# Decay differences on GpSimd, a second buffer for exp(cum), and the second half's HGRN norm in pieces: one change to a two-layer SSD/HGRN2 trunk

## The chip, the cores and the metric

The kernel runs on one core of a Trainium2 chip. The metric is the device time of one execution in microseconds (us). The kernel before was timed in three runs: 2899.86, 2904.77 and 2904.81, median 2904.77. One further execution was profiled, and all rows of profile and trace come from that one.

## The reference

An encoder trunk of two layers, width D = 1024, runs one step over 1024 frames of a new stream (x_prompt) and 32 frames of a running one (x_sample) with the same weights. Layer 0 is a Mamba-2 SSD mixer, layer 1 an HGRN2 mixer; a SwiGLU follows each, and an rmsnorm stands ahead of each of the four and at the end. Cut to what matters:

```python
# SSD, one chunk of frames, per group of 8 heads (4 groups)
cum   = jnp.cumsum(dtc * Ag, axis=1)                  # running sum, never rising: A < 0
seg   = cum[:, :, None] - cum[:, None, :]             # cum_t - cum_s
decay = where(mask, exp(where(mask, seg, 0.0)), 0.0)  # causal: s <= t
xdt   = xc * dtc[..., None]
cb    = einsum('btgn,bsgn->btsg', Cc, Bc)
y = einsum('btsg,btsgh,bsghp->btghp', cb, decay, xdt)
y = y + einsum('btgn,bghpn->btghp', Cc, S) * exp(cum)[..., None]
S = exp(last) * S + einsum('bsgh,bsghp,bsgn->bghpn', exp(last - cum), xdt, Bc)
# gate: yg = (y + D*x) * silu(z), rmsnorm over a group, @ out_w
# HGRN2: h = rmsnorm(x, w); q, f, i, g = split(h @ in_w); gated linear recurrence per head (8 of 128);
#        rmsnorm over a head, * silu(g), @ out_w
```

For s <= t the difference cum_t - cum_s is never above 0, so the exponential may be taken of min(cum_t - cum_s, 0) for all pairs and masked afterwards.

## The kernel before

**Tiling.** Everything lies transposed: features on 128 partitions, frames on the free axis. The frames are cut into two halves: the first of 512 columns, the second of 544 (512 and the 32 of x_sample). Residuals, norms and weights live in SBUF as fp32; a matrix product is made as three passes on TensorE of numbers split into a high and a low part: L314 is high weight by high input, L315 high weight by low input, L316 low weight by high input. ScalarE copies raw weights to their high part (wh<-raw), VectorE subtracts to get the low one (wl<-raw,wh). ScalarE makes all exponentials, Tanh and copies out of PSUM; VectorE the products and sums. L98, L101, L104, L107 and L110 are the lines of the helpers act, tt, stt, ts and dma, so an operation is known by its tiles.

**SSD layer.** Loop over two halves, and in each over four groups of 8 heads. A group has four chunks of 128 frames (in the second half a fifth, of the 32 sample frames). For each chunk:

- `chunk_loads` (L524 on), issued one chunk ahead on SP's queue, brings cum of 8 heads, broadcast over partitions, into two tiles cumB (4 heads each, 128 x 512; tag "cb" of four buffers, so two chunks), and exp(cum) into ec (tag "ec", one buffer). The first chunk of the first half needs no ec.
- `ssd_chunk`: TensorE makes C by B (L552) and transposes x (L557); VectorE makes xdt and xw; ScalarE turns each head's 128 x 128 piece of cumB into a clamped difference with one Relu (scale -1, bias the column cum of the head), then takes one Exp per tile with scale -1; VectorE multiplies with the masked C by B. TensorE transposes B (L572) and ScalarE copies it (Btok, in the trace fixed<-sc 128x128); L579 is C by S, L582 the state product of Btok and xw, L593 the eight products of xdt with the decay tiles, after which the cumB buffers are free.

In the trace an instruction of ScalarE with cumB<-cumB,fixed is such a Relu, one with cumB<-cumB 128x512 the Exp. Among the chunks of a group stand *tasks*: the four z projections of the group (`ssd_z`: a Tanh by ScalarE out of PSUM, z<-mm, then a VectorE operation on it) and the output projections of the group before. After its last chunk comes the gate (`ssd_gate`: squares, a product with ones at L331, Ln, Exp), then the convolution tiles of the next group.

**HGRN layer.** 16 units: two halves, in each eight heads; a unit has four or five chunks (`hgrn_chunk`, `hgrn_chunk_b`, L806 to L825), a gate (`hgrn_gate`: square of the head's output ho, product with ones at L331, Ln, Exp = rstd, two VectorE products, the split into hy), and among its chunks tasks: its own g projection (hg), every second head the output projection of the two heads before (mm<-hy), and the f, q, v projections of the next head. Behind these, in head 6 of the first half, stands the norm of the second half (`norm(1, C_HGN, xns[1], XN2)`): eight squares by ScalarE with seven sums by VectorE, two products with ones (L331), Ln, Exp, and then for each of 8 row blocks a VectorE product, ScalarE's copy (h<-xf) and VectorE's low part.

**What sets the order.** Each engine runs its instructions in a fixed order, which a scheduler writes at build time from priorities and its own costs: program order, with some kinds lifted (L112: norm=600, gate=100, hchunk=50, others 0). Semaphores are placed accordingly. A lifted kind may stand far ahead of where it is written.

Of the kernel before, what the change touches and what calls it, by code (L numbers as in the profile page):

```python
# [11 lines left out]
AF = mybir.ActivationFunctionType  # L12
ALU = mybir.AluOpType
# [9 lines left out]
LEN = (H1, SEQ - H1 + NS)  # L23
# [14 lines left out]
C_SSDN, C_CB, C_FFN, C_HGN, C_GN, C_HG, C_LB = 0, 8, 32, 48, 56, 72, 73  # L38
# [2 lines left out]

TW = 552
FIXED = 14368
BUFS = {"x": 12, "ys": 8, "cb": 4, "xd": 2, "ec": 1, "ss": 1, "xr": 2, "n": 4, "w": 3}
WIDTH = {k: TW for k in BUFS}


@with_exitstack
def trunk_kernel(ctx, tc, x_prompt, x_sample, state_ssd, cache_conv, state_hgrn,
# [5 lines left out]
    V, A, G, PE = nc.vector, nc.scalar, nc.gpsimd, nc.tensor  # L55
# [17 lines left out]
    def slot(tag, s):  # L73
        return T(tag, s, F32R) if isinstance(tag, str) else tag
# [22 lines left out]
    def act(out, in_, f, **kw):  # L97
        A.activation(out=out, in_=in_, func=f, **kw)  # L98
# [7 lines left out]
    def ts(out, a, s1, s2, op0, op1, eng=None):  # L106
        (eng or V).tensor_scalar(out=out, in0=a, scalar1=s1, scalar2=s2, op0=op0, op1=op1)  # L107
# [17 lines left out]
    MUL, ADD, SUB = ALU.mult, ALU.add, ALU.subtract  # L125
# [41 lines left out]
    xr = place(9)  # L167
# [170 lines left out]
    XN = [xnt[:, i] for i in range(16)]  # L338
    XN2 = ["x"] * 12 + ["cb"] * 4
# [39 lines left out]
    @lifted("norm")  # L379
    def norm(h, wc, out, tags, blocks=None, r=None):  # L380

        for (b0, bn) in blocks or ((0, LEN[h]),):
            mmb = BLK[h] if blocks is None else [(0, bn)]
            if r is None:
                r = rstd_of([acc[h][m][:, b0:b0 + bn] for m in range(KD)], mmb, 1.0 / D, bn)
            for m in range(KD):
                xf = T("n", "xf")
                stt(xf[:, :bn], acc[h][m][:, b0:b0 + bn], vc[:, wc + m:wc + m + 1], r[:, :bn], MUL, MUL)
                if m == len(out):
                    out.append((slot(tags[2 * m], "h"), slot(tags[2 * m + 1], "l")))  # L390
                xh, xl = out[m]
                act(xh[:, b0:b0 + bn], xf[:, :bn], AF.Copy)
                tt(xl[:, b0:b0 + bn], xf[:, :bn], xh[:, b0:b0 + bn].bitcast(F32), SUB)
        return out
# [8 lines left out]
    st = [place(TW) for _ in range(NG)]  # L403
# [138 lines left out]
    @lifted("chunk")  # L542
    def ssd_chunk(h, g, c, S, loads, u):
        o, n, smp = CHUNKS[h][c]
        Bt, Ct, xs, Y = u["x"][0], u["x"][1], u["x"][2:], u["Y"]
        cols, elast = dts[h]
        xo = o + (3 if smp else 0)
        Bx, Cx = Bt[:, xo:xo + n], Ct[:, xo:xo + n]
        h0 = g * 8
        cums, ec = loads  # L550
        ps = psum_sc()
        PE.matmul(ps[:n, :n], Bx, Cx, start=True, stop=True)  # L552
        cbm = small("cbm")
        tt(cbm[:n, :n], ps[:n, :n], cmask[:n, :n], MUL)
        ps = psum_sc()
        for j in range(4):
            PE.transpose(ps[:n, j * P:(j + 1) * P], xs[j][:, xo:xo + n], ident)  # L557
        x3 = ps[:n, :].rearrange("p (h q) -> p h q", q=64)
        xdt, xw = T("xd", "xdt")[:, :512], T("xd", "xw")[:, :512]
        tt(xdt[:n, :].rearrange("p (h q) -> p h q", q=64), x3,  # L560
           cols[:n, c, h0:h0 + 8].unsqueeze(2).to_broadcast([n, 8, 64]), MUL)
        tt(xw[:n, :].rearrange("p (h q) -> p h q", q=64), x3,
           cols[:n, c, 64 + h0:64 + h0 + 8].unsqueeze(2).to_broadcast([n, 8, 64]), MUL)
        for q in range(2):
            cb3 = cums[q]
            for i in range(4):
                hh = 32 + h0 + 4 * q + i
                act(cb3[:n, i, :n], cb3[:n, i, :n], AF.Relu, scale=-1.0, bias=cols[:n, c, hh:hh + 1])
            act(cb3[:n, :, :n], cb3[:n, :, :n], AF.Exp, scale=-1.0)
            tt(cb3[:n, :, :n], cb3[:n, :, :n], cbm[:n, :n].unsqueeze(1).to_broadcast([n, 4, n]), MUL)  # L570
        ps = psum_sc()
        PE.transpose(ps[:n, :P], Bx, ident)  # L572
        Btok = small("Btok")
        act(Btok[:n, :], ps[:n, :P], AF.Copy)
        if ec is not None:
            y2 = psum_sc()
            y23 = y2.rearrange("p (j t) -> p j t", t=P)
            for j in range(4):
                PE.matmul(y23[:, j, :n], S[:, j * P:(j + 1) * P], Cx, start=True, stop=True)  # L579
            tt(ec[:, :, :n], y23[:, :, :n], ec[:, :, :n], MUL)  # L580
        pp = psum_sc()
        PE.matmul(pp, Btok[:n, :], xw[:n, :], start=True, stop=True)  # L582
        if ec is None:
            V.tensor_copy(S, pp)
        else:
            S3 = S.rearrange("p (h q) -> p h q", q=64)
            tt(S3, S3, elast[:, h0:h0 + 8, c:c + 1].to_broadcast([P, 8, 64]), MUL)
            tt(S, S, pp, ADD)
        y1 = psum_sc()
        y13 = y1.rearrange("p (j t) -> p j t", t=P)  # L590
        for i in range(8):
            r = 64 * (i % 2)
            PE.matmul(y13[r:r + 64, i // 2, :n], xdt[:n, i * 64:(i + 1) * 64], cums[i // 4][:n, i % 4, :n],  # L593
                      start=True, stop=True)
        yo = Y[:, :, o:o + n]
        if ec is None:
            act(yo, y13[:, :, :n], AF.Copy)
        else:
            tt(yo, y13[:, :, :n], ec[:, :, :n], ADD)
# [260 lines left out]
    def hgrn_layer(after):  # L860
        units = [(h, e) for h in range(2) for e in range(8)]
        us = [{"S": None} for _ in units]
        for f in (hgrn_f, hgrn_q, hgrn_v):
            f(0, 0, us[0])
        for i, (h, e) in enumerate(units):
            u = us[i]
            tasks = [lambda: hgrn_g(h, e, u)]
            if e % 2 == 0 and i:
                ph, pe = units[i - 1]
                tasks += [lambda m4=m4: hgrn_out(ph, pe // 2, m4, [us[i - 2]["y"], us[i - 1]["y"]])  # L870
                          for m4 in range(2)]
            if i + 1 < len(units):
                nh, ne = units[i + 1]
                tasks += [lambda f=f: f(nh, ne, us[i + 1]) for f in (hgrn_f, hgrn_q, hgrn_v)]
            if (h, e) == (0, 6):
                tasks.append(lambda: norm(1, C_HGN, xns[1], XN2))
            if (h, e) == (1, 6):
                tasks += after[:1]
            if (h, e) == (1, 7):
                tasks += after[1:]  # L880
            u["o"] = T("ys", "ho")
            if e % 2 == 0:
                yt = sp.tile([P, 4 * TW], F32R, tag="Y", bufs=1, name=nm("hy"))[:, :4 * LEN[1]]
                yp = yt.rearrange("p (j t) -> p j t", j=4)
            u["yp"] = yp
            nch = len(CHUNKS[h])
            for c in range(nch):
                second = hgrn_chunk(h, e, c, u)
                q = -(-len(tasks) // (nch - c))
                for i2, t in enumerate(tasks[:q]):  # L890
                    if i2 == HB2:
                        second()
                    t()
                if q <= HB2:
                    second()
                tasks = tasks[q:]
            hgrn_gate(h, e, u)
        return [lambda m4=m4: hgrn_out(1, 3, m4, [us[-2]["y"], us[-1]["y"]]) for m4 in range(2)]
# [6 lines left out]
    def x_stat(h, keep):  # L905

        return rstd_of([acc[h][m][:, :LEN[h]] for m in range(KD)], BLK[h], 1.0 / D, LEN[h], keep)

    def norm_pieces(h, wc, out, blocks, r):

        def piece(m, b0, bn):
            xf = T("n", "xf")
            stt(xf[:, :bn], acc[h][m][:, b0:b0 + bn], vc[:, wc + m:wc + m + 1], r[:, b0:b0 + bn], MUL, MUL)
            if m == len(out):
                out.append((XN[2 * m], XN[2 * m + 1]))
            xh, xl = out[m]
            act(xh[:, b0:b0 + bn], xf[:, :bn], AF.Copy)
            tt(xl[:, b0:b0 + bn], xf[:, :bn], xh[:, b0:b0 + bn].bitcast(F32), SUB)
        return [lambda m=m, b=b: piece(m, *b) for b in blocks for m in range(KD)]
# [209 lines left out]
    def mixed(a, b):  # L1129

        out, k = [], 0
        for i, x in enumerate(a):
            out.append(x)
            while k < len(b) and k * len(a) < (i + 1) * len(b):
                out.append(b[k])
                k += 1
        return out + b[k:]
# [98 lines left out]
    xns, dts = [[], []], [None, None]  # L1236
# [22 lines left out]
    due, r = mixer_ffn(hgrn_layer, 1, C_FFN + 8, False)  # L1259
# [41 lines left out]
```

## Time and profile before

| What | Value |
| --- | --- |
| median of three runs | 2904.77 us |
| lowest, highest run | 2899.86, 2904.81 us |
| profiled execution, own time | 2906.18 us |
| its span | 2904.4 us |
| TensorE (PE) | 2848.8 us busy, 98% |
| VectorE (DVE) | 2152.7 us, 74% |
| ScalarE (ACT) | 1559.5 us, 54% |
| GpSimd (POOL) | 46.4 us, 2%, 156 instructions |
| granted TensorE clock, mean | 0.996 |
| DMA | 282.61 MB, mean 97 GB/s |

A row of a timeline or of waits reads: start in us of the span, duration, engine, line, operation, tile written <- tiles read, shapes, count, and in brackets the idle time just before it in us with what ended it. A row of groups has busy time and mean duration in ns. A row of stretches has, for each engine, busy us and count, then the granted clock (1.00 is full), the share of DMA and GB/s. Names stand without their number, so that z<-mm is any tile of z.

### The profile page before, as it was taken

What the parts mean: (1) busy time and instruction counts of PE and PEld (TensorE: products, weight loads), DVE (VectorE), ACT (ScalarE), POOL (GpSimd) and SP (SyncE); (2) the same over time, 40 slices, a digit from 0 to 9 for tenths busy, and PEclk for the clock granted to TensorE, in tenths of its full rate; (3) what the DMA queues carried; (4) which work ended last, traced back from release to release, by engine and by line L of the source; (5) the groups of instructions that cost most, each with busy time, mean ns of one, the idle gap of its engine ahead of it and who ended that gap; (6) DMA issues with size and microseconds to landing.
All of it is one profiled execution on the core that took longest, in us unless ns stands there. A gap on an engine that the chain in (4) does not pass through costs nothing. (4 is left out here: it accounts for less than half of the span.)

```text
span 2904.4 us, 49072 instructions
## 1 busy us (share of the span) xinstructions
PE 2848.8 (98%) x19711; PEld 2619.9 (90%) x19711; DVE 2152.7 (74%) x3744; ACT 1559.5 (54%) x2922; POOL 46.4 (2%) x156
## 2 busy tenths in 40 slices
PE   8999999999999999999999999999999999999998
PEld 7777788999988999999999888899988999999998
DVE  6777787777787977887777455655568877887777
ACT  6645645554653754456544655655554644554445
POOL 0000000000000000000000000000000000000000
PEclk9999999999999999999999999999999999999999
DMA  5443434344332333323333222222222332333223
GB/s 151 115 111 92 110 82 120 109 114 108 107 90 88 102 111 100 102 80 95 109 95 105 81 82 73 60 79 77 74 84 81 119 100 88 120 94 94 90 88 111
DMA packets 401247, 282.61 MB, mean 97 GB/s; under 512 B 22633, under 2 KB 388730, under 8 KB 401018
## 3 DMA queue, kind: packets, MB, share of 16 engines
q1 hardware_dynamic: 401018, 279.47, 33.2%
q8 instruction: 154, 2.52, 0.3%
q14 instruction: 75, 0.61, 0.1%
HBM read 271.61 MB, written 7.82 MB: 96 GB/s over the span
## 5 line engine op out<-in xcount | busy, mean ns | idle before, releaser
L98 ACT ACTIVATE wh<-raw 128x512 fp32r<-128x512 f32 (+1 forms) x688 | 557.3, 818 | 541.8 <-PE mm L315 419.5
L314 PE MATMUL mm<-xn,wh 128*128 128x272 f32 (+2 forms) x1552 | 524.8, 338 | 0.3 <-ACT wh L98 0.3
L315 PE MATMUL mm<-xn,wh 128*128 128x272 f32 (+2 forms) x1552 | 519.1, 335 | 3.8 <-issue 3.8
L316 PE MATMUL mm<-xn,wl 128*128 128x272 f32 (+2 forms) x1552 | 518.5, 334 | 3.2 <-DVE wl L101 3.2
L101 DVE TENSOR_TENSOR wl<-raw,wh 128x1024 fp32r<-128x1024 f32 x308 | 375.9, 1222 | 83.7 <-ACT wh L98 63.5
L101 DVE TENSOR_TENSOR fixed<-mm,fixed 128x272 f32<-128x272 f32 (+1 forms) x512 | 262.9, 525 | 192.7 <-PE mm L316 191.1
L314 PE MATMUL mm<-fh,wh 128*128 128x272 f32 (+1 forms) x1056 | 341.7, 325 | 1.1 <-DVE fixed L101 0.8
L315 PE MATMUL mm<-fl,wh 128*128 128x272 f32 (+1 forms) x1056 | 341.9, 324 | 0.7 <-DVE fl L101 0.7
L316 PE MATMUL mm<-fh,wl 128*128 128x272 f32 (+1 forms) x1056 | 341.7, 324 | 0.0
L316 PEld LDWEIGHTS mm<-xn,wl 128*128 128x128 f32 x1552 | 293.0, 189 | 37.3 <-issue 6.0
L314 PEld LDWEIGHTS mm<-xn,wh 128*128 128x128 f32 x1552 | 293.0, 189 | 29.5 <-issue 2.6
L315 PEld LDWEIGHTS mm<-xn,wh 128*128 128x128 f32 x1552 | 293.0, 189 | 27.1 <-issue 0.8
L101 DVE TENSOR_TENSOR wh<-raw,wh 128x512 fp32r<-128x512 f32 x380 | 257.1, 688 | 38.5 <-ACT wh L98 35.2
L989 PE MATMUL mm<-th,wh 128*128 128x272 f32 (+1 forms) x912 | 260.4, 286 | 0.1
L990 PE MATMUL mm<-tl,wh 128*128 128x272 f32 (+1 forms) x912 | 259.7, 285 | 0.0
L991 PE MATMUL mm<-th,wh 128*128 128x272 f32 (+1 forms) x912 | 259.6, 285 | 0.0
L314 PEld LDWEIGHTS mm<-fh,wh 128*128 128x128 f32 x1056 | 198.4, 188 | 17.4 <-DVE fixed L101 1.7
L315 PEld LDWEIGHTS mm<-fl,wh 128*128 128x128 f32 x1056 | 198.7, 188 | 16.3 <-DVE fl L101 1.8
L316 PEld LDWEIGHTS mm<-fh,wl 128*128 128x128 f32 x1056 | 198.7, 188 | 15.3
L989 PE MATMUL sc<-xn,wh 128*128 128x272 f32 (+1 forms) x608 | 173.2, 285 | 0.5 <-ACT wh L98 0.5
L989 PEld LDWEIGHTS mm<-th,wh 128*128 128x128 f32 x912 | 171.8, 188 | 1.9 <-ACT s L98 1.2
L990 PE MATMUL sc<-xn,wh 128*128 128x272 f32 (+1 forms) x608 | 173.2, 285 | 0.0
(251 smaller groups left out, 6637.0 us busy)
## 6 DMA issues: line engine op xcount, KB each, us to landing
raw<-in_ffn_w_down_dram SPq DMA_DIRECT2D x90, 512.0 KB, 3.5
raw<-in_ffn_w_gate_dram SPq DMA_DIRECT2D x88, 512.0 KB, 3.8
raw<-in_ffn_w_up_dram SPq DMA_DIRECT2D x88, 512.0 KB, 4.6
raw<-in_ssd_in_w_dram SPq DMA_DIRECT2D x80, 512.0 KB, 4.0
raw<-in_hgrn_in_w_dram SPq DMA_DIRECT2D x64, 512.0 KB, 4.2
cumB<-cumd SPq DMA_DIRECT2D x64, 256.0 KB, 4.5
raw<-in_ssd_out_w_dram SPq DMA_DIRECT2D x32, 512.0 KB, 3.5
raw<-in_hgrn_out_w_dram SPq DMA_DIRECT2D x16, 512.0 KB, 3.3
```

The source lines that it names most:

```text
L98: A.activation(out=out, in_=in_, func=f, **kw)
L101: (eng or V).tensor_tensor(out=out, in0=a, in1=b, op=op)
L314: PE.matmul(ps[:, :bn], a, mh, start=(k == 0), stop=False)
L315: PE.matmul(ps[:, :bn], a, ml, start=False, stop=False)
L316: PE.matmul(ps[:, :bn], b, mh, start=False, stop=(k == n - 1))
L989: PE.matmul(ps[:, :n], a, mh, start=(k == 0 and not more), stop=False, skip_group_check=True)
L990: PE.matmul(ps[:, :n], a, ml, start=False, stop=False, skip_group_check=True)
L991: PE.matmul(ps[:, :n], b, mh, start=False, stop=(k == 3), skip_group_check=True)
```

## The change

It has three parts. **One:** the clamped differences of the SSD chunks (256 pieces of 128 x 128 and 32 of 32 x 32) are made by GpSimd, by one tensor_scalar each (subtract the column, then minimum with 0) instead of a Relu on ScalarE; the sign is now that of the difference itself, so Exp has scale 1. **Two:** the tag "ec" has two buffers. **Three:** the norm of the second half for HGRN is no longer one call in head 6 of the first half. Its statistics (`x_stat`, kept in st[2]) are a task at the end of head 5; its eight row blocks (`norm_pieces`) are mixed among the tasks of head 6, and `norm_pieces` gets the tags of the tiles it writes. Neither of the two carries the priority of `norm`.

```diff
-BUFS = {"x": 12, "ys": 8, "cb": 4, "xd": 2, "ec": 1, "ss": 1, "xr": 2, "n": 4, "w": 3}
+BUFS = {"x": 12, "ys": 8, "cb": 4, "xd": 2, "ec": 2, "ss": 1, "xr": 2, "n": 4, "w": 3}
@@ -565,8 +565,8 @@  ssd_chunk
             cb3 = cums[q]
             for i in range(4):
                 hh = 32 + h0 + 4 * q + i
-                act(cb3[:n, i, :n], cb3[:n, i, :n], AF.Relu, scale=-1.0, bias=cols[:n, c, hh:hh + 1])
-            act(cb3[:n, :, :n], cb3[:n, :, :n], AF.Exp, scale=-1.0)
+                ts(cb3[:n, i, :n], cb3[:n, i, :n], cols[:n, c, hh:hh + 1], 0.0, SUB, ALU.min, G)
+            act(cb3[:n, :, :n], cb3[:n, :, :n], AF.Exp)
             tt(cb3[:n, :, :n], cb3[:n, :, :n], cbm[:n, :n].unsqueeze(1).to_broadcast([n, 4, n]), MUL)
@@ -860,6 +860,7 @@  hgrn_layer
         us = [{"S": None} for _ in units]
+        r = []
@@ -872,8 +873,10 @@
                 tasks += [lambda f=f: f(nh, ne, us[i + 1]) for f in (hgrn_f, hgrn_q, hgrn_v)]
+            if (h, e) == (0, 5):
+                tasks.append(lambda: r.append(x_stat(1, st[2])))
             if (h, e) == (0, 6):
-                tasks.append(lambda: norm(1, C_HGN, xns[1], XN2))
+                tasks = mixed(tasks, norm_pieces(1, C_HGN, xns[1], ((0, LEN[1]),), r[0], XN2))
@@ -906,13 +909,13 @@
-    def norm_pieces(h, wc, out, blocks, r):
+    def norm_pieces(h, wc, out, blocks, r, tags=XN):
 
         def piece(m, b0, bn):
             xf = T("n", "xf")
             stt(xf[:, :bn], acc[h][m][:, b0:b0 + bn], vc[:, wc + m:wc + m + 1], r[:, b0:b0 + bn], MUL, MUL)
             if m == len(out):
-                out.append((XN[2 * m], XN[2 * m + 1]))
+                out.append((slot(tags[2 * m], "h"), slot(tags[2 * m + 1], "l")))
             xh, xl = out[m]
```

**The order, ScalarE in group 1 of the SSD layer's first half.** cumB_1857 and cumB_1859 are the two cumB tiles of the group's fourth chunk, z_1829 is a z tile, fixed<-sc_1888 the copy of the transposed B of the third chunk, wh_2072 a weight copy. Before:

```order
L98 ACTIVATE cumB_1857<-cumB_1857,fixed 128x128 x4
L98 ACTIVATE cumB_1859<-cumB_1859,fixed 128x128
L98 ACTIVATE cumB_1857<-cumB_1857 128x512
L98 ACTIVATE z_1829<-mm_1830 128x512
L98 ACTIVATE fixed<-sc_1888 128x128
L98 ACTIVATE cumB_1859<-cumB_1859,fixed 128x128 x3
L98 ACTIVATE wh_2072<-raw_2070 128x1024
L98 ACTIVATE cumB_1859<-cumB_1859 128x512
```

With the change (cumB_1769 and cumB_1771 are the tiles of the third chunk, sc_1800 is the B of the second):

```order
L98 ACTIVATE z_1741<-mm_1742 128x512
L98 ACTIVATE fixed<-sc_1800 128x128
L98 ACTIVATE cumB_1769<-cumB_1769 128x512
L98 ACTIVATE cumB_1771<-cumB_1771 128x512
L98 ACTIVATE cumB_1857<-cumB_1857 128x512
L98 ACTIVATE cumB_1859<-cumB_1859 128x512
L98 ACTIVATE z_1829<-mm_1830 128x512
L98 ACTIVATE wh_2072<-raw_2070 128x1024
L98 ACTIVATE fixed<-sc_1888 128x128
```

For the second chunk z and the copy of B stand ahead of the next chunk's two Exps; for the third they stand behind both. GpSimd, which had only small copies and memsets there, now has:

```order
L488 MEMSET pre_2076 128x3
L107 TENSOR_SCALAR cumB_1769<-cumB_1769,fixed 128x128 x4
L107 TENSOR_SCALAR cumB_1771<-cumB_1771,fixed 128x128 x4
L107 TENSOR_SCALAR cumB_1857<-cumB_1857,fixed 128x128 x4
L107 TENSOR_SCALAR cumB_1859<-cumB_1859,fixed 128x128 x4
L107 TENSOR_SCALAR cumB_2329<-cumB_2329,fixed 128x128 x4
L107 TENSOR_SCALAR cumB_2331<-cumB_2331,fixed 128x128 x4
```

Each Exp follows the four differences of its own tile.

**The order, HGRN layer, first half.** ScalarE at the end of head 5, before (ho_18531 is the head's output, sq_18747 and rstd_18749 belong to its gate, hy_18228 is its result for the output projection):

```order
L98 ACTIVATE ho_18531<-sc_18741 128x128
L98 ACTIVATE sq_18747<-ho_18531 128x512
L98 ACT_TABLE_LOAD
L98 ACTIVATE rstd_18749<-sc_18750,fixed 128x512
L98 ACTIVATE hkv_18766<-sc_18763 128x256
L98 ACT_TABLE_LOAD
L98 ACTIVATE rstd_18749<-rstd_18749 128x512
L98 ACTIVATE wh_18903<-raw_18901 128x1024
L98 ACTIVATE hy_18228<-ho_18531 128x512
```

With the change the statistics of the second half (fixed<-sc,fixed 128x272 twice: Ln; fixed<-fixed 128x544: Exp) stand just ahead of the gate of head 5:

```order
L98 ACT_TABLE_LOAD
L98 ACTIVATE fixed<-sc_18762,fixed 128x272
L98 ACTIVATE fixed<-sc_18765,fixed 128x272
L98 ACTIVATE ho_18531<-sc_18771 128x128
L98 ACT_TABLE_LOAD
L98 ACTIVATE fixed<-fixed 128x544
L98 ACTIVATE sq_18777<-ho_18531 128x512
L98 ACTIVATE hg_18798<-mm_18805 128x512
L98 ACTIVATE hkv_18796<-sc_18793 128x256
L98 ACT_TABLE_LOAD
L98 ACTIVATE rstd_18779<-sc_18780,fixed 128x512
L98 ACTIVATE ho_18788<-sc_18834 128x128
```

Behind these follow, up to hy_18228<-ho_18531, one ACT_TABLE_LOAD, the Exp of rstd_18779, a second hkv copy, the copies of the first two row blocks (h_18840, h_18846), a weight copy and one ho copy. On TensorE eleven 512-column matmuls and three 128-column ones stand between the second L331 of the statistics (sc_18765) and the gate's (sc_18780). The first product that reads the new hy comes 28 rows behind the gate's L331; the last rows ahead of it are:

```order
L314 MATMUL mm_18916<-hy_18228,wh_18912 128x512
L315 MATMUL mm_18916<-hy_18228,wh_18912 128x512
L316 MATMUL mm_18916<-hy_18228,wl_18913 128x512
L821 MATMUL sc_18902<-hkv_18894 128x128
L823 MATMUL sc_18904<-fixed,hkv_18894 128x128
L825 MATMUL sc_18904<-hq_18639,fixed 128x128
L806 MATMUL sc_19005<-hq_18639,hk_18615 128x128
L810 MATMUL sc_19008<-fixed,hk_18615 128x128
L811 MATMUL sc_19008<-fixed,hv_18690 128x128
L314 MATMUL mm_18856<-hy_18228,wh_18852 128x512
```

The products of hy_18228 ahead of its last row read the part that head 4 wrote; the chunk products of head 6 (L806 to L825) stand among them.

## Prediction

> **What bounds the kernel now.** I read the page's busy line and chain first, then busy time by stretches, then who TensorE waited for, and last the timelines of two places.
>
> ```profile
> PE 2848.8 (98%) x19711; PEld 2619.9 (90%) x19711; DVE 2152.7 (74%) x3744; ACT 1559.5 (54%) x2922; POOL 46.4 (2%) x156
> ```
>
> TensorE (PE) is the bound: of a span of 2904.4 us it is idle for 55.6. A change that adds and removes no matmul can only move that idle time and the clock. Where it lies, by stretches (after the first comma: busy us of PE, PEld, DVE, ACT, POOL, each with its count; then the granted clock, DMA share, GB/s):
>
> ```profile
> 180.00:280.00 100.00, 94.19 (x467) 73.99 (x466) 71.94 (x102) 50.98 (x93) 3.91 (x12) 1.00 0.38 104
> 280.00:380.00 100.00, 95.30 (x471) 74.50 (x469) 70.69 (x102) 53.36 (x98) 4.06 (x13) 1.00 0.37 99
> ...
> 460.00:860.00 400.00, 399.01 (x3087) 369.17 (x3086) 312.73 (x509) 218.60 (x476) 18.88 (x74) 1.00 0.39 104
> 1820.00:1860.00 40.00, 35.83 (x187) 30.70 (x186) 27.08 (x43) 28.83 (x44) 0.00 (x0) 0.91 0.18 53
> ```
>
> The first half of the SSD layer loses 5 us in 100; the second half (460 to 860) loses 1.0 in 400, so there is nothing to win there; and 40 us in HGRN, where the second half's norm stands, lose 4.2 and run at a clock of 0.91. In the first half TensorE waited, between 90 and 430 us, for:
>
> ```profile
> PE sc L582 <- ACT wh L98: 5.0, 4, 1.7
> PE sc L582 <- DVE xw L101: 3.3, 3, 1.4
> ...
> PE sc L579 <- ACT fixed L98: 1.0, 1, 1.0
> PE sc L582 <- ACT fixed L98: 1.0, 1, 1.0
> ```
>
> L582 is the state product of a chunk. It needs xw from VectorE and the transposed B from ScalarE, and both are late there.
>
> **The chunk loop of the first half.** Here is one turn, for the third chunk of group 1. The load for the chunk *after* it is issued by SP at 189.30, when the product L593 of the chunk *before* has freed two of the four cumB buffers; it lands as ScalarE's wait ends:
>
> ```profile
> 189.30 0.91 SPq L110 DMA_DIRECT2D cumB<-cumd  x2
> ```
>
> ```profile
> 193.52 1.70 ACT L98 ACTIVATE cumB<-cumB,fixed 128x128 f32<-128x128 f32 x5 [5.51 <-DMA cumB<-cumd]
> 195.13 0.61 ACT L98 ACTIVATE cumB<-cumB 128x512 f32<-128x512 f32 x1
> 195.65 0.58 ACT L98 ACTIVATE z<-mm 128x512 f32<-128x512 f32 x1
> 196.13 0.27 ACT L98 ACTIVATE fixed<-sc 128x128 f32<-128x128 f32 x1
> ```
>
> ```profile
> 196.26 0.69 DVE L104 SCALAR_TENSOR_TENSOR z<-z,mm 128x512 f32<-128x512 f32 x1 [1.36 <-ACT z L98]
> ```
>
> ```profile
> 187.58 0.67 PE L582 MATMUL sc<-xw,fixed 128*128 128x512 f32 x1 [1.72 <-ACT wh L98]
> ...
> 198.29 1.10 PE L582 MATMUL sc<-xw,fixed 128*128 128x512 f32 x2 [1.16 <-ACT wh L98]
> ```
>
> So the turn is a loop: state product (187.58), L593, load issued (189.30), landed (about 193.5), five Relus and one Exp, z (195.65), on VectorE z, xdt, xw, and the next state product (198.29). From landing to product are 4.8 us. z and B stand behind work on a load that they do not need.
>
> **The second buffer for ec: 0.** It frees SP from waiting for Y before an ec load. But the cumB load that drives the loop waits for L593 and its own four buffers, which stay; it is issued no sooner. No row shows TensorE waiting for ec. Bounds: -1 to 0.
>
> **The Relus leave ScalarE.** 256 of 128x128 (and 32 small ones) go, at this price:
>
> ```profile
> L98 ACT ACTIVATE cumB<-cumB,fixed 128x128 f32<-128x128 f32 x256 | 85.5, 392 | 59.1 <-DMA cumB<-cumd 51.5 <-PE mm L315 6.9 <-DVE cumB L101 0.3
> ```
>
> 85 us of an engine that is busy 54% of the time are worth nothing in themselves. What counts is where the Exps now stand. In three places ScalarE's new order puts B's copy ahead of the next Exps, and the wait goes: group 1's second chunk (1.72 above), group 0's last (the 1.0 of L582 <- ACT fixed), group 3's third (the 1.0 of L579). That is -3.7.
>
> In six others the order printed above has both Exps ahead of z, and z now waits until GpSimd has done *all eight* differences, instead of five Relus. The trace has no such GpSimd instruction, only neighbours:
>
> ```profile
> 9.88 0.29 POOL L149 TENSOR_SCALAR_AFFINE_SELECT fixed<-fixed 128x128 f32<-128x128 f32 x1
> 10.12 0.10 POOL L488 MEMSET pre<- 128x3 f32 x1
> ...
> 439.92 0.66 POOL L491 COPY pre<-fixed 128x3 f32<-128x3 f32 x1
> ...
> 449.25 0.18 POOL L504 COPY fixed<-pre 128x3 f32<-128x3 f32 x1
> 449.37 0.18 POOL L490 COPY pre<-fixed 128x3 f32<-128x3 f32 x1
> ```
>
> The nearest is the select: same size, one input, in place, the next instruction starting 0.24 later. I take 0.25 for one difference. The lower bound is 0.12, the spacing of two 3-column copies; the upper 0.66, the same copy where it took longest in this stretch. Eight take 2.0; I add 0.6 once, for one VectorE instruction that holds GpSimd up (0.66 less the 0.18 of the undisturbed copy, rounded up), 0.15 for the handover, and 0.6 for the second Exp. z starts 3.35 after the landing instead of 2.13 (195.65 less 193.52), and everything behind it is 1.2 later. B now also stands behind a weight copy, but VectorE's three operations still end later. Four chunks pay 1.2 (group 1's and group 2's third and fourth); group 2's second, where the load's second half lands late anyway, and group 3's second, behind one Exp only, I put at 0.7. Sum: 4 x 1.2 + 2 x 0.7 = 6.2, less 3.7: **+2.5**. With 0.12 for a difference each of the six gains 1.0 on that (-3.7 in all); with 0.66 each loses 3.3 more (+22).
>
> At the end of a group the next group's differences land in the middle of the gate, and the squares for L331 stand behind their Exps. The squares lose the eight Relus and gain GpSimd's time, so I put 0, between -2 and +3.
>
> The Trainium skill (SBUF — State Buffer, section Who interferes with whom) says that a VectorE instruction with two SBUF inputs and a GpSimd instruction that reads SBUF exclude each other for the whole of an instruction. The two prices of one copy, 0.18 and 0.66, fit that; by this rule, carried through all eight, the price is that of the slower rival below.
>
> Second SSD half: z comes from TensorE later than the load lands and the new order has z first, so there is only the 1.0 idle of the row above to win: **-0.5** (-1 to 0). VectorE delayed by GpSimd elsewhere: **+0.5** (0 to 3; VectorE has a fourth of its time free).
>
> **HGRN's norm.** What it costs now:
>
> ```profile
> 1844.44 0.77 PE L314 MATMUL mm<-h,wh 128*128 128x272 f32 x4 [3.15 <-ACT h L98]
> 1845.83 0.57 PE L314 MATMUL mm<-h,wh 128*128 128x272 f32 x1 [0.62 <-DVE hg L104]
> ```
>
> ```profile
> 1844.00:1848.00 4.00, 2.94 (x12) 2.46 (x13) 4.00 (x6) 2.43 (x4) 0.00 (x0) 0.65 0.00 0
> 1848.00:1852.00 4.00, 4.00 (x20) 4.00 (x20) 4.00 (x8) 1.84 (x3) 0.00 (x0) 0.50 0.45 135
> ```
>
> 3.8 of waiting, and behind it a clock of 0.65 and 0.50 for 4 us each: 1.4 + 2.0 lost, less 0.3 in which it waited anyway: 6.9 in all. The pieces, a head sooner, are done before the first product that reads them: -6.9.
>
> But the statistics now stand a head sooner too, and directly ahead of that head's gate. Their length is seen before, from the second L331 to the end of the Exp:
>
> ```profile
> 1838.84 0.39 PE L331 MATMUL sc<-sq,fixed 128*128 128x272 f32 x1
> ```
>
> ```profile
> 1840.93 1.28 ACT L98 ACT_TABLE_LOAD   x1
> 1842.22 0.66 ACT L98 ACTIVATE rstd<-rstd 128x544 f32<-128x544 f32 x1
> ```
>
> 4.0 us; then the gate's square (0.6). TensorE has between that L331 and the gate's L331 eleven 512-wide matmuls at 0.23 and three small pairs at 0.22, 3.4 with the L331 itself: idle 1.2. From the gate's L331 to its hy took before:
>
> ```profile
> 1797.17 1.02 PE L331 MATMUL sc<-sq,fixed 128*128 128x512 f32 x2
> ```
>
> ```profile
> 1802.68 0.63 ACT L98 ACTIVATE hy<-ho 128x512 fp32r<-128x512 f32 x1 [0.60 <-DVE ho L101]
> ```
>
> 5.5 to its start, 6.1 to its end. Now hg, a second kv copy, two pieces and a weight copy stand in that chain, about 2.5 more: 8.6. TensorE has 5.9 of work until the first product that reads this hy (thirteen 512-wide, the gate's L331, eleven small pairs): idle 2.7. The new waits are **3.9** (0 if the copies slide into gaps; 7 if the clock falls here as well), and the step is **-3.0**.
>
> The Trainium skill (TensorE: Matmul & The Clock Gate, Part 1) says that the clock is halved after an idle window of about 3.4 us and restored after a busy one. The trace agrees: 3.15 us idle, then about 6.8 us at half. By that rule waits of 1.2 and 2.7 stay below it.
>
> **Sum:** 2.5 - 0.5 + 0.5 - 3.0 = -0.5 on the profiled execution, whose own time is 2906.2 (1.8 around the span). That one is 1.4 over the median of the runs shown, 2904.8; I put the same difference there: **2904.2 us**. This measurement can tell about 0.2%, 5.8 us, from no change.
>
> **Rivals.**
>
> *The losses do not come* (28%). A difference costs nearer 0.12 than 0.25, or the new HGRN waits fall into gaps. For it: ScalarE is half idle. With 0.15 the six chunks gain 4.8, with half the new HGRN waits 2: 2904.2 - 6.8 = about 2897. Against it: ScalarE is in order, and its order is written.
>
> *GpSimd is held up by VectorE* (27%), the slower side. VectorE has many instructions with both inputs in SBUF, and a 3-column copy took 0.66 beside them. If each of the eight waits for one of these, a difference costs 0.5 to 0.66 and the six chunks pay 2.0 to 3.3 more each: 2904.2 + 12 to 20 = 2916 to 2924. It decides from about 0.38 a difference on, where 6 x 8 x 0.13 = 6.2 is added. Against it: in the loop VectorE is itself idle, waiting for z.
>
> *The edit does nothing where it should* (within the forecast): the ec buffer removes no wait, and Exp behind GpSimd takes the place of Relu behind DMA.
>
> **How the numbers follow.** Forecast (no change) 45%, faster 28%, slower 27%. The range, 2893 to 2917, takes in the faster rival with its bounds and the slower one's beginning; the forecast's own range is 2899 to 2910.
>
> **What would show it.** Right: POOL's TENSOR_SCALAR near 0.25 apart; in 180 to 400 us the waits at L582 in fewer chunks but over 2 us each, z waiting behind an Exp that waits for GpSimd; no wait at mm<-h near 1844 and no clock below 1 there, but waits at L331 and at mm<-hy some 25 to 35 us sooner. Wrong: L582's waits gone (the loop is not what I think), TENSOR_SCALAR at 0.5 or more, TensorE waiting in the second SSD half, or no new wait ahead of hy.

## The result, and the profile after

| | median | lowest to highest | ratio to before, 95% interval |
| --- | --- | --- | --- |
| before | 2903.53 us | 2898.69 to 2906.57 | |
| changed | 2972.61 us | 2969.36 to 2976.18 | 1.0241 [1.0227, 1.0254] |

The change costs 69 us. The forecast was 2904.2, in a range from 2893 to 2917; the measured time lies far above that range. The profiled executions have spans of 2904.4 and 2970.2, so they show the difference. The busy line of the changed kernel's page, and, from its groups with the shapes kept apart, the one of the large differences:

```profile
PE 2872.0 (97%) x19711; PEld 2633.2 (89%) x19711; DVE 2156.6 (73%) x3744; ACT 1477.7 (50%) x2634; POOL 290.6 (10%) x444
```

```profile
L107 POOL TENSOR_SCALAR cumB<-cumB,fixed 128x128 f32<-128x128 f32 x256 | 230.5, 918 | 276.7 <-DMA cumB<-cumd 205.3 <-DVE xf L104 30.5 <-DVE fixed L101 14.3
```

ScalarE lost the 82 us that were to leave it, GpSimd took up 244. A 128x128 difference took 0.918 us on average, where the forecast has 0.25 and an upper bound of 0.66. TensorE is busy 23 us longer with the same 19711 matmuls, and its granted clock was 0.986 on average where it was 0.996.

**Where.** Both kernels have as many matmuls, so the start of the n-th can be compared in the two traces. The changed kernel is 54.4 later at the 2400th (the end of the SSD layer's first half, 453 us before), 70.9 at the 6000th (behind the SSD layer), 69.6 at the 11500th (HGRN, head 3), 3.3 more at the 12000th, and 6.7 less by the 12500th. So the HGRN part gives back 3.4, and the SSD layer takes 71. The same two stretches of matmuls of the SSD layer (500th to 2000th and on to the 5500th), by stretches, before:

```profile
83.00:395.60 312.60, 298.30 (x1506) 232.84 (x1504) 237.19 (x362) 176.53 (x341) 12.88 (x39) 0.99 0.38 102
395.60:856.50 460.90, 455.25 (x3504) 420.79 (x3502) 367.76 (x588) 252.22 (x537) 26.68 (x94) 1.00 0.40 108
```

and after:

```profile
83.00:443.80 360.80, 316.06 (x1500) 243.33 (x1498) 239.84 (x363) 142.96 (x229) 96.44 (x143) 0.92 0.32 88
443.80:927.10 483.30, 463.56 (x3502) 425.86 (x3502) 369.84 (x588) 206.56 (x369) 175.29 (x262) 0.98 0.39 102
```

The first stretch is 48.2 longer: TensorE's idle time went from 14.3 to 44.7 (+30.4), its busy time for the same work from 298.3 to 316.1 (+17.8), at a clock of 0.92. The second is 22.4 longer: +14.1 idle, +8.3 busy. Of these 70.6 us, 44.5 are waiting and 26 are longer busy time for the same work. The lower clock is enough for the 26: in the SSD layer TensorE is now busy for 59 us at half clock, before for 3, and half of the difference is 28. What TensorE waited for after, 90 to 465 us:

```profile
PE sc L582 <- DVE xw L101: 24.5, 6, 5.8
PE sc L331 <- DVE sq L101: 16.4, 3, 7.6
PE mm L314 <- ACT wh L98: 4.5, 1, 4.5
PE sc L579 <- ACT fixed L98: 3.3, 1, 3.3
PE sc L582 <- ACT fixed L98: 1.4, 1, 1.4
```

Of the six waits at L582 for xw, five are 3.7 to 5.8 us long and the last 1.1; three gates wait at L331 for 4.2 to 7.6. The 4.5 at L314 are a weight copy (wh) that stands behind the Exps of group 3's last chunk. Here is the chunk whose turn the prediction shows, after the change (timeline):

```profile
195.64 6.00 POOL L107 TENSOR_SCALAR cumB<-cumB,fixed 128x128 f32<-128x128 f32 x8 [1.51 <-PE mm L316]
...
201.67 0.63 ACT L98 ACTIVATE cumB<-cumB 128x512 f32<-128x512 f32 x1 [2.13 <-POOL cumB L107]
202.20 0.58 ACT L98 ACTIVATE z<-mm 128x512 f32<-128x512 f32 x1
202.81 0.69 DVE L104 SCALAR_TENSOR_TENSOR z<-z,mm 128x512 f32<-128x512 f32 x1 [5.89 <-ACT z L98]
204.85 2.05 PE L582 MATMUL sc<-xw,fixed 128*128 128x512 f32 x2 [5.77 <-DVE xw L101]
...
208.01 1.39 SPq L110 DMA_DIRECT2D cumB<-cumd  x2
```

The order is the forecast one: differences, second Exp, z, VectorE, state product. Only the eight differences last 6.0 instead of 2.0. The product that waited 1.16 now waits 5.77, and behind this wait the clock is halved (the two L582 took 1.10 before and take 2.05 here):

```profile
204.00:208.00 4.00, 3.15 (x14) 1.68 (x16) 4.00 (x7) 0.00 (x0) 0.00 (x0) 0.50 0.00 0
```

Shorter waits can do the same. This is a gate of the second half, with the wait before its product and the stretch behind it:

```profile
704.75 0.79 PE L331 MATMUL sc<-sq,fixed 128*128 128x272 f32 x1 [2.52 <-DVE sq L101]
...
704.70:708.10 3.40, 3.35 (x11) 2.92 (x12) 3.14 (x4) 3.35 (x6) 0.32 (x3) 0.50 0.16 51
```

At the end of a group the squares of the gate stand behind the differences of the next group (timeline of group 1's end):

```profile
227.39 7.05 POOL L107 TENSOR_SCALAR cumB<-cumB,fixed 128x128 f32<-128x128 f32 x8 [10.13 <-DVE Y L101]
...
234.47 0.63 ACT L98 ACTIVATE cumB<-cumB 128x512 f32<-128x512 f32 x1 [2.13 <-POOL cumB L107]
235.01 0.58 ACT L98 ACTIVATE z<-mm 128x512 f32<-128x512 f32 x1
235.49 1.14 ACT L98 ACTIVATE sq<-Y 128x512 f32<-128x512 f32 x2
...
241.30 1.19 PE L331 MATMUL sc<-sq,fixed 128*128 128x512 f32 x1 [4.19 <-DVE sq L101]
```

In HGRN, TensorE's waits after the change, 1850 to 1990 us; there is none left at mm<-h, and the clock is 1.00 where it was 0.91:

```profile
PE sc L331 <- ACT sq L98: 1.9, 2, 1.0
PE sc L810 <- ACT ho L98: 1.0, 1, 1.0
PE sc L821 <- ACT hkv L98: 0.8, 1, 0.8
```

### The profile page after: what moved, and what is told of

Same layout as the page of the kernel before. It is cut to its first block, busy times and chain, and to the rows that moved or that the text cites. A ratio compares the mean times of both kernels' runs of the same rounds, so it can differ in the third digit from the quotient of the medians.

```text
span 2970.2 us, 49211 instructions
## 1 busy us (share of the span) xinstructions
PE 2872.0 (97%) x19711; PEld 2633.2 (89%) x19711; DVE 2156.6 (73%) x3744; ACT 1477.7 (50%) x2634; POOL 290.6 (10%) x444
## 4 chain that ended last, share of the span: by engine, by line
PE 85%; DVE 5%; POOL 4%; ACT 3%; issue 2%; DMA 1%; SPq 0%; DVEq 0%; POOLq 0%; ACTq 0%
PE mm L314 17%; PE mm L315 17%; PE mm L316 17%; PE mm L994 5%; PE mm L992 5%; PE mm L993 5%; PE sc L994 4%; PE sc L992 4%; PE sc L993 4%; POOL cumB L107 4%; DMA cumB<-cumd 1%; PE sc L331 1%; PE sc L582 1%; PE sc L593 1%; DVE fixed L101 1%
## 5 line engine op out<-in xcount | busy, mean ns | idle before, releaser
L314 PE MATMUL mm<-xn,wh 128*128 128x272 f32 (+2 forms) x1552 | 529.2, 341 | 6.6 <-ACT wh L98 4.5
L316 PE MATMUL mm<-xn,wl 128*128 128x272 f32 (+2 forms) x1552 | 521.1, 336 | 0.9 <-DVE wl L101 0.9
L314 PE MATMUL mm<-fh,wh 128*128 128x272 f32 (+1 forms) x1056 | 341.8, 325 | 1.0 <-DVE fixed L101 0.7
L316 PE MATMUL mm<-fh,wl 128*128 128x272 f32 (+1 forms) x1056 | 341.6, 324 | 0.0
L314 PEld LDWEIGHTS mm<-xn,wh 128*128 128x128 f32 x1552 | 295.7, 191 | 37.2 <-issue 5.5
L316 PEld LDWEIGHTS mm<-xn,wl 128*128 128x128 f32 x1552 | 294.8, 190 | 34.1 <-issue 5.6
L107 POOL TENSOR_SCALAR cumB<-cumB,fixed 128x128 f32<-128x128 f32 (+1 forms) x288 | 248.1, 879 | 283.4 <-DMA cumB<-cumd 208.3
L314 PEld LDWEIGHTS mm<-fh,wh 128*128 128x128 f32 x1056 | 198.3, 188 | 17.6 <-DVE fixed L101 1.7
L316 PEld LDWEIGHTS mm<-fh,wl 128*128 128x128 f32 x1056 | 198.6, 188 | 15.1
L992 PE MATMUL sc<-xn,wh 128*128 128x272 f32 (+1 forms) x608 | 173.1, 285 | 0.5 <-ACT wh L98 0.5
```

The lines of the kernel that those rows point to most:

```text
L314: PE.matmul(ps[:, :bn], a, mh, start=(k == 0), stop=False)
L316: PE.matmul(ps[:, :bn], b, mh, start=False, stop=(k == n - 1))
L992: PE.matmul(ps[:, :n], a, mh, start=(k == 0 and not more), stop=False, skip_group_check=True)
```

## The experiments

The theory that these rows suggest (A in the expectations): *the differences cost 0.7 us each of GpSimd's own time, and since z, the copy of B and the gate's squares stand behind their Exps, TensorE waits for them and loses clock*. Rivals: VectorE holds GpSimd up (B); another part of the change has a share (C); any other engine than ScalarE would do the same harm (D); GpSimd is too slow wherever the Exps stand (E).

### One part at a time

pool_alone: only the `ts(..., SUB, ALU.min, G)` and the Exp of the diff. ec_alone: only `"ec": 2`. hgrn_alone: only the lines in hgrn_layer and norm_pieces.

> Only the differences move to GpSimd; ec keeps one buffer and the HGRN norm stays as it was. Theory A (the whole loss is GpSimd's eight differences standing ahead of the Exps): +69 (the whole change) +4 (the HGRN part, which in the traces gave back 3.3 - 6.7 = -3.4) = +70 to +75 on the kernel before, about 2975; TENSOR_SCALAR at 0.71 us where nothing disturbs it. Theory C (the second ec buffer or the HGRN part carries a share of the loss): less than +60.

> Only the second ec buffer. Theory A: nothing, -1 to +1. Theory C (SP's queue runs on to ec loads and delays a cumB or weight load behind them): +3 to +15, with longer times from issue to landing or later issues of cumB.

> Only the HGRN part: statistics at the end of head 5, pieces in head 6. By the traces of the whole change: -3.4 (the wait at the first mm<-h and the halved clock behind it go, -6.7; new waits at the gate of head 5, +3.3). Rival: the gain is tied to the shifted SSD layer and is absent here, 0.

| run | median | ratio, 95% interval | SSD layer | HGRN norm |
| --- | --- | --- | --- | --- |
| pool_alone | 2978.04 | 1.0262 [1.0248, 1.0276] | +70.4 | -0.6 |
| ec_alone | 2901.85 | 0.9999 [0.9989, 1.0008] | -4.1 | -1.0 |
| hgrn_alone | 2899.93 | 0.9994 [0.9985, 1.0003] | -2.4 | +3.4, then -6.8 |

The last two columns compare the starts of the same matmuls with those of the kernel before (0 to the 6000th; 11500th to 12500th). Runs in which nothing of the SSD layer, or only ec, was changed differ there by 2 to 4, so less than that means nothing in that column. The whole loss is in the differences (pool_alone: +76 by the ratio, +70 to +75 expected); the second ec buffer does nothing; the HGRN part moves what it moved in the whole change, too little for the timed runs to tell from none.

### The price of a difference

prices: behind the last output, on tiles that nobody needs any more (cut):

```diff
...
+    for w in (32, 128, 256, 512):
+        for k in range(4):
+            ts(A0[:, :w], A0[:, :w], col, 0.0, SUB, ALU.min, G)
+    for k in range(4):
+        tt(A0[:, :128], A0[:, :128], A0[:, 128:256], SUB, G)
...
+    for k in range(12):
+        tt(A2[:, :512], A2[:, :512], A3[:, :512], ALU.max)
+    for k in range(12):
+        ts(A0[:, :128], A0[:, :128], col, 0.0, SUB, ALU.min, G)
```

> The kernel before with a tail behind its last output that only measures: on GpSimd tensor_scalar (subtract a column, minimum with 0) of 128 x 32, 128, 256 and 512 in place, a tensor_tensor of 128 x 128, the same on VectorE and a Relu on ScalarE, and then twelve of GpSimd's beside twelve VectorE operations with two SBUF inputs of 512. Theory A (the price is the instruction's own): 128 x 128 at 0.71 with VectorE idle, and a large part of it fixed: 0.5 to 0.6 at 32 columns. Theory B (the price is VectorE's hold on GpSimd): 0.3 with VectorE idle, 0.7 and more beside it. The time of this kernel says nothing.

The tail's groups (line, engine, operation, shapes, count, busy, mean ns), the row of all its tensor_scalars by the tile (shortest, median, longest in ns), and from the timeline the four undisturbed 128x128 and the last ones with their VectorE neighbours:

```profile
L107 POOL TENSOR_SCALAR fixed<-fixed 128x512 f32<-128x512 f32 x4 | 8.0, 1992 | 0.4
L107 POOL TENSOR_SCALAR fixed<-fixed 128x256 f32<-128x256 f32 x4 | 4.6, 1139 | 0.4
L101 POOL TENSOR_TENSOR fixed<-fixed 128x128 f32<-128x128 f32 x4 | 1.8, 452 | 0.3
L98 ACT ACTIVATE fixed<-fixed 128x128 f32<-128x128 f32 x4 | 1.6, 401 | 21.6 <-DVE fixed L107 21.6
L107 DVE TENSOR_SCALAR fixed<-fixed 128x128 f32<-128x128 f32 x4 | 1.1, 286 | 18.7 <-POOL fixed L101 18.6
```

```profile
L107 POOL TENSOR_SCALAR fixed<-fixed x31: 392/712/1997, 2891.6 to 2930.4; 128x128 f32<-128x128 f32 x17, 128x512 f32<-128x512 f32 x6, 128x32 f32<-128x32 f32 x4, 128x256 f32<-128x256 f32 x4
```

```profile
2897.75 3.13 POOL L107 TENSOR_SCALAR fixed<-fixed 128x128 f32<-128x128 f32 x4
...
2920.19 10.88 POOL L107 TENSOR_SCALAR fixed<-fixed 128x128 f32<-128x128 f32 x13 [3.92 <-DVE fixed L101]
2920.94 9.52 DVE L101 TENSOR_TENSOR fixed<-fixed 128x512 f32<-128x512 f32 x12 [0.92 <-POOL fixed L107]
```

From 256 to 512 columns are 853 ns, 3.33 ns a column; four of 128 columns in 3.13 us with VectorE idle are one in 0.80, 0.71 of it busy. That is GpSimd's own price, and it is theory A's. The fixed part is smaller than expected: the shortest, of 32 columns, took 0.39, not 0.5 to 0.6. Beside VectorE twelve of the thirteen took the same 0.71 and one 1.21. In the changed kernel's trace the 85 differences that have no VectorE operation beside them all took 0.71, the other 171 took 1.02 on average, single ones up to 2.8. So theory B may have a part there, about 53 of the 230 us, but the larger part of the price is there without VectorE.

### Another engine, and half the dose

on_vector: the same call without `G`. half_pool:

```diff
+                if q:
+                    act(cb3[:n, i, :n], cb3[:n, i, :n], AF.Relu, scale=-1.0, bias=cols[:n, c, hh:hh + 1])
+                else:
                     ts(cb3[:n, i, :n], cb3[:n, i, :n], cols[:n, c, hh:hh + 1], 0.0, SUB, ALU.min, G)
-            act(cb3[:n, :, :n], cb3[:n, :, :n], AF.Exp)
+            act(cb3[:n, :, :n], cb3[:n, :, :n], AF.Exp, scale=-1.0 if q else 1.0)
```

> The whole change, but the 288 differences on VectorE instead of GpSimd: same operation, same place in the program. VectorE took 0.286 us for one alone against GpSimd's 0.712 (run prices), so eight take 2.6 instead of 6.0 and more. Theory A (GpSimd's own price ahead of the Exps makes the loss): nearly all of the +69 goes, -4 to +8 on the kernel before, with 2.5 us more VectorE work per chunk as the remaining cost. Theory D (taking the differences away from ScalarE at all, so that each Exp waits for another engine, makes the loss): +40 or more.

> The whole change, but only the first four heads of a chunk on GpSimd, the other four as Relus on ScalarE. Theory A: the Exp of the first tile waits 3.0 to 3.7 instead of both for 6.0 to 7.4, the second for four Relus; the waits at L582 mostly stay below 3.4 us and the clock full: +10 to +25 on the kernel before. A loss in proportion to the number of GpSimd instructions would be +33.

on_vector: 2923.17, ratio 1.0074 [1.0059, 1.0089], +22: neither the -4 to +8 of theory A nor the +40 or more of D. half_pool: 2934.89, 1.0110 [1.0095, 1.0126], +32 by the ratio, the proportional value and not the lower one; a full clock had been expected there, and it was halved behind nine waits of 2.0 to 4.7 us. TensorE's waits, 85 to 470 us, of on_vector, with the group of its differences and, from the timeline, its longest wait; then those of half_pool:

```profile
PE mm L316 <- DVE wl L101: 13.4, 3, 9.2
PE sc L582 <- DVE xw L101: 6.7, 7, 1.9
...
L107 DVE TENSOR_SCALAR cumB<-cumB,fixed 128x128 f32<-128x128 f32 x256 | 57.9, 281 | 24.3 <-DMA cumB<-cumd 24.3
...
451.35 0.59 PE L316 MATMUL mm<-xn,wl 128*128 128x272 f32 x1 [9.23 <-DVE wl L101]
```

```profile
PE sc L585 <- DVE xw L101: 16.2, 6, 4.3
PE sc L331 <- DVE sq L101: 11.3, 3, 4.7
```

On VectorE the waits at L582 fall from 24.5 to 6.7: at 0.28 a difference the loop is no longer a problem. But a loss of 22 is left, and not where it was expected. VectorE now stands still for 24.3 us at differences whose load has not landed, nearly all of it in the chunks between 185 and 320 us; yet there (1000th to 2000th matmul) the kernel falls behind by only 4. Some 10 are lost in one place, between the 2200th and the 2250th, where the low part of a weight (wl, made at 450.08) stands behind 12 us of VectorE's work without a pause, on the gate, the convolution and dt. No difference stands in that stretch, and why that order came out so was not tried. So this run shows that the loop's loss goes with the price; what the rest of its 22 us is due to stays open.

### The load earlier

pool_ahead: cumB is loaded two chunks ahead, with `"cb": 6` (ec one ahead as before). act_ahead: the same with Relus on ScalarE, ec in two buffers and the HGRN part.

```diff
-                nxt = chunk_loads(h, g, c + 1, False) if c + 1 < nch else None
+                if c + 2 < nch:
+                    cums.append(chunk_loads(h, g, c + 2, False))
+                nec = ec_loads(h, g, c + 1, False) if c + 1 < nch else None
```

> The whole change with all differences on GpSimd, but cumB loaded two chunks ahead into six buffers instead of one ahead in four, so the differences can be done a chunk earlier. Theory A (latency inside the loop load - difference - Exp - z - state product - next load): the waits at L582 between 180 and 460 us go, 40 to 60 of the +69 with them: +10 to +30. Rival (GpSimd's throughput, or its holding up VectorE, is what costs): the loss stays above +50, since the same 288 instructions run beside the same VectorE work.

> The kernel before with the HGRN part of the change, Relus on ScalarE, and cumB two chunks ahead in six buffers. Theory A: the loop of the kernel before is broken as well; the 10.3 us that it waits at L582 and L579 between 90 and 430 us shrink to under half: -5 to -8, with the HGRN part's -3.4 in all -8 to -11, about 2893. Rival (the scheduler uses the earlier loads to put still more Relus and Exps ahead of z): no gain over the HGRN part alone.

pool_ahead: 2982.51, 1.0287 [1.0268, 1.0307], ten more than the change itself, where +10 to +30 was expected. act_ahead: 2905.28, 1.0011 [1.0003, 1.0020], no gain, where -8 to -11 was expected. The theory as it stood, latency inside the loop, failed; the rival that GpSimd's throughput is what costs would fit pool_ahead as well, and falls only with the next experiment. The timeline of pool_ahead says why:

```profile
203.69 0.91 SPq L110 DMA_DIRECT2D cumB<-cumd  x2
...
207.50 5.76 POOL L107 TENSOR_SCALAR cumB<-cumB,fixed 128x128 f32<-128x128 f32 x8 [0.95 <-DMA cumB<-cumd]
...
213.29 0.63 ACT L98 ACTIVATE cumB<-cumB 128x512 f32<-128x512 f32 x1 [2.12 <-POOL cumB L107]
213.83 0.58 ACT L98 ACTIVATE z<-mm 128x512 f32<-128x512 f32 x1
...
216.47 1.19 PE L587 MATMUL sc<-xw,fixed 128*128 128x512 f32 x1 [4.99 <-DVE xw L101]
```

The new load serves a chunk later, but the written order moved with it: the Exps of the newest load stand ahead of z again, and z again starts 6.3 after the landing. More buffers only made the work that z doesn't need lie further ahead. So the theory has to be (A2 in the expectations): **price times order**. That is tested by leaving the price and changing only the order.

### The order

pool_order is the whole change, in which the Exps get a bias of zeros that VectorE makes from what they must stand behind; `u["prev"]` is one column of the last gate's rstd (cut):

```diff
+    def behind(u, c):
+        if c >= 2 and len(u["z"]) >= 2:
+            a, b = u["z"][-2][:, 0:1], u["B"][:, 0:1]
+        elif c < 2 and u["prev"] is not None:
+            a = b = u["prev"]
+        else:
+            return None
...
+        stt(zero, a, 0.0, b, MUL, MUL)
...
-            act(cb3[:n, :, :n], cb3[:n, :, :n], AF.Exp)
+            act(cb3[:n, :, :n], cb3[:n, :, :n], AF.Exp, **({"bias": zero[:n, 0:1]} if zero is not None else {}))
```

pool_order_z leaves out `u["prev"]`; pool_order_stat also moves x_stat to head 2 (`tasks.insert(2, ...)`); relu_order has the bias of zeros, but Relus on ScalarE and one ec buffer.

> The whole change with all 288 differences on GpSimd, and one thing added: the Exps of a chunk are made to stand behind the z of two chunks before and the copy of B of the chunk before, and the Exps of a group's first two chunks behind the rstd of the last gate. That is done with a dependency: their bias is a column of zeros that a small VectorE operation makes from z and B, or from rstd (32 more such operations of one column, exact zeros). GpSimd's price stays as it is. Theory A2 (the price hurts only because the written order puts the Exps of the newest load ahead of z, B and the gate's squares): the waits at L582 and L331 between 90 and 460 us go, the SSD layer's +70 falls to between -8 and +8. Theory E (GpSimd's 6 to 7 us per chunk are too long wherever the Exps stand, since the products L593 then wait for the decay tiles): +30 or more stays, as waits at L593.

> As pool_order, and the statistics of the second half's HGRN norm are a task in the middle of head 2 instead of at the end of head 5. In the traces of the whole change the new waits at the end of head 5 cost +3.3. If they come from the statistics' squares, Ln and Exp ahead of that head's gate, they fall to about 1 (only the two first pieces remain in the gate's chain), and the time is 1 to 3 below pool_order; if they come from the pieces, nothing changes.

> The kernel before with the HGRN part (statistics at the end of head 5) and the forced order of the Exps, but the differences stay Relus on ScalarE. Their own place can't be forced in this way, and the order has six or more of the next chunk's Relus ahead of z still, where the first waits for the load. Theory A2 (what stands ahead of z and waits decides, on whichever engine): the waits at L582 stay near the 10.3 us of before, and the time near the HGRN part alone: -6 to 0 on the kernel before. If the order of the Exps by itself made the gain of pool_order, the time is near that one's, -10.

> As pool_order (differences on GpSimd), but only the Exps of a group's third and later chunks are held back behind z and B; those of its first two chunks may again stand ahead of the last gate's squares. Theory A2: the waits at L331 come back (16.4 us in three places of the first half of the whole change, 7.3 in the second, and the halved clock behind those over 3.4 us), the ones at L582 don't: +25 to +35 on pool_order. If the waits at L582 alone made the loss: within 5 of pool_order.

| run | median | ratio, 95% interval | SSD layer | HGRN norm |
| --- | --- | --- | --- | --- |
| pool_order | 2892.40 | 0.9965 [0.9951, 0.9979] | -9.3 | +3.3, then -6.7 |
| pool_order_stat | 2888.28 | 0.9949 [0.9937, 0.9962] | -7.6 | 0.0, then -7.4 |
| relu_order | 2906.83 | 1.0019 [1.0010, 1.0029] | +2.3 | +3.3, then -6.6 |
| pool_order_z | 2941.91 | 1.0141 [1.0126, 1.0157] | +36.8 | +4.6, then -6.8 |

With the same 288 instructions on GpSimd the SSD layer went from +71 to -9, and the kernel is 0.35% faster than the one before. The first half gains 14.7 (to the 2400th matmul); 5 are lost again at the start of the second half, around a wait of 2.1 at L314 that the whole change has in the same place, and pool_order_stat and pool_order_z too. TensorE's waits of pool_order, 85 to 470 us, and the stretch that answers to the first one above, with a clock of 1.00 and 2.6 idle:

```profile
PE mm L316 <- DVE wl L101: 2.8, 3, 1.4
PE sc L475 <- ACT pre L98: 1.5, 1, 1.5
PE sc L331 <- DVE sq L101: 1.4, 1, 1.4
PE sc L599 <- ACT cumB L98: 1.2, 1, 1.2
PE sc L599 <- ACT fixed L98: 1.0, 1, 1.0
```

```profile
83.00:380.60 297.60, 294.98 (x1503) 231.28 (x1501) 240.39 (x375) 145.40 (x229) 113.90 (x143) 1.00 0.40 108
```

A chunk's turn there: the differences take as long as ever (7.5 us), and TensorE doesn't wait for them.

```profile
196.70 7.52 POOL L107 TENSOR_SCALAR cumB<-cumB,fixed 128x128 f32<-128x128 f32 x8 [0.93 <-DMA cumB<-cumd]
...
198.34 0.58 ACT L98 ACTIVATE z<-mm 128x512 f32<-128x512 f32 x1
198.81 0.27 ACT L98 ACTIVATE fixed<-sc 128x128 f32<-128x128 f32 x1
```

Theory E (too slow wherever the Exps stand) falls. Without the part for the gates (pool_order_z) 49.5 of the gain are gone, more than the 25 to 35 expected; its waits:

```profile
PE sc L331 <- DVE sq L101: 17.8, 3, 7.1
PE sc L599 <- DVE xw L101: 9.5, 2, 5.1
```

The next group's Exps now stand ahead of the group's last two z as well as of the squares, so two waits at the state product (L599 in that kernel) came back too, which the expectation left out. relu_order is 0.2% slower than before, where -6 to 0 us was expected: the Relus stay ahead of z. With the differences on ScalarE this order is worth nothing; with them on GpSimd, it is the whole difference between a loss and a gain. pool_order_stat is the fastest of all kernels run, 14.8 under its before and 4.1 under pool_order, where 1 to 3 were expected. The new waits at the end of head 5 are gone in its trace (the +3.3), with two pieces still ahead of hy, so they came from the statistics and not from the pieces.

## Why the prediction was wrong, and where it was right

- **The bound and the loop: right.** TensorE waits in six chunks because z or the copy of B stands behind the Exps, and those behind GpSimd. The three waits that were to go are gone, and the six chunks that were to pay are those that wait, 3.3 to 5.8 each ("the waits at L582 in fewer chunks but over 2 us each"; group 3's second chunk waits at L579 instead). Not forecast were 1.4 and 1.1 in the third chunks of groups 0 and 3, and the 4.5 for the weight copy.
- **The price of a difference: the step that failed.** "I take 0.25 for one difference", after an affine select of the same size, upper bound 0.66 after a copy at its slowest. The runs show 0.71 for one alone, 0.80 from start to start, 0.918 in the kernel. Even the upper bound was too low. With 0.71 the prediction's own sum gives 4 x (1.2 + 8 x 0.46) + 2 x (0.7 + 8 x 0.46) = 28.3, less 3.7, +25 instead of +2.5. (A small term is loose too: 0.66 less 0.18 is 0.48, not 0.6, which is worth 0.7 in the sum.) The waits at L582 and L579 rose from 10.3 to 29.2, +19.
- **The gate: mis-sized.** "so I put 0, between -2 and +3" rested on the same price. The waits at L331 went from 2.8 to 16.4 in the first half, with 7.3 in the second, where there were none.
- **The clock: left out of this sum.** The working used the halved clock for HGRN, where a wait goes, and not for the waits that the upper bound of the price would bring. Ten waits of 3.3 to 7.6 us between 110 and 465 us halved it, and three of 2.1 to 2.5 in the second half; about 26 of the 70.6 us are lost in this way. The rule cited there (the Trainium skill, TensorE: Matmul & The Clock Gate, Part 1: about 3.4 us of idle halve the clock) fits the ten: behind 5.77 idle the trace shows 0.50 for 4 us. The three shorter ones don't fit it (0.50 for 3.4 us behind the 2.52 shown above), nor does one in the kernel before, of 1.98 at 128.06. Behind a wait of 2.23 at 596.50 and one of 1.01 in HGRN the clock stayed full. So in these traces the length of a wait alone doesn't decide it, and what else does was not tried. The step that took a wait of 2.7 in HGRN for free had less room than it says; the waits that came there were too short to show it.
- **Second SSD half, -0.5: wrong, +16.5** (2400th to 6000th matmul). For the chunk loop the reason given holds, 0.6 at L582. But the trace has 7.3 at the three gates, which that step doesn't have, 2.6 more at the start of the half (L314 and L316; the 1.5 at L475 were there before), and three times 3.4 us of half clock, worth about 5.
- **VectorE delayed elsewhere, +0.5:** not seen apart from the rest; its busy time rose from 2152.7 to 2156.6.
- **The ec buffer, 0:** right (0.9999).
- **HGRN, -3.0:** right in size, -3.4 (forecast -6.9 and +3.9; measured -6.7 and +3.3). The place is half wrong: 1.0 at the gate's L331 as forecast (1.2), but nothing at mm<-hy, where 2.7 were expected; instead hkv, ho and the next head's square came late by 0.8 to 1.0 each. The chain from that L331 to the end of hy took 9.1 us, near the 8.6 forecast, and the first product that reads hy started as it ended; the waits came at products ahead of that one.
- **The rival on the slower side** had the right place, but took VectorE for the cause and 0.5 to 0.66 for the price. The price was for the most part GpSimd's own (0.71 of 0.918); pool_order shows that the place was a matter of order.

## What to carry to other kernels

In this kernel, work that moved to a slower engine cost little where nobody stood behind it, and much where an in-order engine in the middle (here ScalarE, with its Exps) waited for it ahead of what the bound engine needed next. Read that from the written order first, and if it is so, change the order before the engine. When no row shows an operation, the row of another operation of the same size is no price: take an upper end that a slow engine can really reach, and carry it through the sum with everything that then follows, the clock too. More buffers didn't mend an order that puts the newest load's work first.

## What the runs showed of the hardware

GpSimd's tensor_scalar (a column and a constant, fp32) takes 0.39 us for 32 columns, 0.71 for 128, 1.14 for 256 and 1.99 for 512, about 0.29 and 3.3 ns a column, where VectorE takes 0.29 for 128. A GpSimd tensor_tensor of 128 columns, with two inputs, took only 0.45, less than the tensor_scalar with one.

GpSimd and VectorE in the prices run: beside twelve VectorE operations of two SBUF inputs GpSimd's started every 0.81, as they do alone (one took 1.21 instead of 0.71); VectorE's started every 0.81 as well and took 0.77 each instead of 0.69. A pair one after the other would need 1.40. By the rule that the prediction cited (the Trainium skill, SBUF — State Buffer, Who interferes with whom) the two exclude each other for a whole instruction; in that run they don't. In the kernel, where VectorE's operations follow each other at 0.6, single differences of 1.2 to 2.8 would fit it. What makes the difference between the two was not tried and stays open.
